# Conv and gate columns of a hybrid decoder step by pairs in seven block products

## The chip, the cores and the metric

The kernel runs on one core of a Trainium2 chip. A core has TensorE (matrix products; in the profile PE, its weight loads PEld), VectorE (DVE), ScalarE (ACT), GpSimd (POOL) and SyncE (SP), each with a queue of its own that it works off in order, and 16 DMA engines. Transfers are issued by SP and by Pool. The metric is the time of one execution on the device in microseconds (us).

## The reference, cut to what matters

One step of a decoder layer for 560 tokens: 16 meta tokens, 512 prompt tokens and 32 sample tokens (8 sequences of 4). The model width is 2048; attention and convolution have 1024 channels.

```
h = rmsnorm(x, g_pre)
q, k, v, ga, cb, cc, ch, gc, ma, mc = jnp.split(h @ w_in, split_offsets(), axis=-1)
a = attend(q, k, v, b_sb).reshape(bsz, t, D_ATTN) * jax.nn.silu(ga)
u = cc * ch
u_ext = jnp.concatenate([conv_hist.astype(u.dtype), u], axis=1)
c = cb * causal_conv(u_ext, w_conv, b_conv) * jax.nn.silu(gc)
merged = (jax.nn.sigmoid(ma + b_gate[:D_MODEL]) * (a @ w_pa)
          + jax.nn.sigmoid(mc + b_gate[D_MODEL:]) * (c @ w_pc))
y = x + rmsnorm(merged @ w_out, g_post)
```

Columns q to gc are 1024 wide each, ma and mc 2048. The attention has 8 heads of 128 and is stick-breaking: a weight is a sigmoid times the product of (1 - sigmoid) of all later keys before the query, computed by sums of softplus. Sample tokens also attend to 512 cached keys of their sequence, in four pages of 128 that a page table names. All is float32. The meta tokens' outputs are dropped.

## The kernel before

**Products.** Channels lie on the partitions, tokens along the free axis. A number is kept as hi + lo, and a product is three matmuls: whi by hi, whi by lo, wlo by hi. A weight tile is a block of 1024 rows by 128 columns (512 KB): weights() (L180 to L191) loads it on SP into one of three raw tiles, ScalarE casts hi (L188), VectorE subtracts to get lo (L189), four such pairs at most. A column tile of h @ w_in takes two such blocks: for each of two halves of the tokens (a PSUM block each; some 272 columns), 16 contraction tiles with three matmuls (gemm_into, L201). That is 96 matmuls per column tile. PSUM has three blocks for such products (mm), three for logits (z), one for o and one for transposes.

**Order.** RMSNorm and its split into h_hi, h_lo; the ga columns; eight heads (head(), L336 to L465: K, V and Q columns, logits L396, softplus, sums L450, product with V L460, result to a_scr in DRAM L465); then conv_in(0), whose columns stand beside the last head; the gate columns (L659 to L666); convolution; a @ w_pa and c @ w_pc by pairs of column tiles (L716 to L735); the output product (16 column tiles for tokens below 288, the rest by token, L796 to L840) and the last norm. A scheduler lays the instructions of each engine out in advance; each engine then keeps that order.

**Decode.** decode_steps() is a generator, and dec_step() advances it beside the projections. Each of 32 pages of keys (512 KB, Pool queue, L527 to L535) is multiplied with the four queries of its sequence (qb, q rows broadcast to all partitions, L546): for two queries by a VectorE product 1024 wide (pr, L553) that ScalarE sums by head (junk, L556), for two by VectorE product-and-sum by head (prod, L560). This lies at the gate columns, one step for each column tile. Then softplus and exponent of the logits, and 32 pages of values with 128-row products (L631), beside the columns of the convolution.

**Gates and convolution.** A gate tile is sigmoid of its PSUM block, and goes to gate_scr in DRAM by Pool (L666). conv_in(i) makes cc and ch columns, their product u and the three taps; later gc and cb columns (L684 to L691) finish c in SBUF (c_raw), which is split into c_hl (L703). a_hl is read back from a_scr two tiles at a time beside the last four of these (arl).

Of the kernel before, what the change touches and what calls it, by code (L numbers as in the profile page):

```python
# [8 lines left out]
F32 = mybir.dt.float32  # L9
F32R = mybir.dt.float32r  # L10
# [15 lines left out]
MID = 288                # tokens [.., MID) and [MID, T) go to two PSUM banks  # L26
ALL = ((0, MID), (MID, T))
QRY = ((NMETA, MID), (MID, T))           # tokens whose outputs are asked for
CNV = ((NMETA - 2, MID), (MID, T))       # these and the conv history before them
TQ = T - NMETA           # 544  # L30
PQ = SEQ                 # prompt tokens among them
# [5 lines left out]
EPS = 1e-6  # L37
LNEXP = "natural_log_exp_and_others"
# [6 lines left out]
def hybrid_step_kernel(  # L45
# [38 lines left out]
    # -------------------------------------------------------------- constants  # L84
# [17 lines left out]
    def load_x(xt, i):  # L102
        lo, hi = XT[i]
        if i == 0:
            nc.sync.dma_start(xt[0:NMETA, :], meta_tokens)
            nc.sync.dma_start(xt[NMETA:hi, :], xp[0:hi - NMETA, :])
        elif hi <= TP:
            nc.sync.dma_start(xt, xp[lo - NMETA:hi - NMETA, :])
        else:
            nc.sync.dma_start(xt[0:TP - lo, :], xp[lo - NMETA:SEQ, :])  # L110
            nc.sync.dma_start(xt[TP - lo:hi - lo, :], xs)
# [21 lines left out]
    # g_pre on every partition, by a product with ones  # L133
# [85 lines left out]
    def parts(outs, ranges, base=0):  # L219
        """(PSUM block, slice of a tile whose column 0 is token `base`) of each range."""  # L220
        return [(o, slice(t0 - base, t1 - base)) for o, (t0, t1) in zip(outs, ranges)]

    # the first two gates start on the first tokens while the others are normalized
    START = ((NMETA, 2 * P), (2 * P, T))
# [21 lines left out]
    # small tables: per-channel columns by a transpose of row-wise loads  # L246
# [88 lines left out]
    def head(h):  # L335
# [18 lines left out]
        for ob, s in parts(o, ALL):  # L354
            act.copy(vr[:, s], ob)
# [515 lines left out]
```

## Time and profile before

| | |
|---|---|
| median of 3 runs | 1734.3 us (1733.22 to 1734.79) |
| span of the profiled execution | 1736.9 us |
| TensorE busy | 1706.4 us, 12764 matmuls recorded |
| VectorE, ScalarE, GpSimd busy | 842.8, 744.7, 202.2 us |
| DMA, mean over the span | 249.87 MB, 144 GB/s |

The profiled execution is 2.6 us above the median of the timed runs. A row of instruction groups reads: line of the kernel, engine, operation, output<-inputs, shapes, count | busy us, mean ns of one | idle time of the engine just before them, and what ended most of it. A row of a window has its start and end, its length, then busy us and count for PE, PEld, DVE, ACT and POOL, the granted clock of TensorE (1.00 is full), the mean share of the DMA engines, and GB/s. A row of the timeline has start, length, engine, line, operation and tiles. Matmuls overlap in the pipeline, so their rate is read from counts in a window, not from the length of one.

### The profile page before, as it was taken

What the parts mean: (1) busy time and instruction counts of PE and PEld (TensorE: products, weight loads), DVE (VectorE), ACT (ScalarE), POOL (GpSimd) and SP (SyncE); (2) the same over time, 40 slices, a digit from 0 to 9 for tenths busy, and PEclk for the clock granted to TensorE, in tenths of its full rate; (3) what the DMA queues carried; (4) which work ended last, traced back from release to release, by engine and by line L of the source; (5) the groups of instructions that cost most, each with busy time, mean ns of one, the idle gap of its engine ahead of it and who ended that gap; (6) DMA issues with size and microseconds to landing.
All of it is one profiled execution on the core that took longest, in us unless ns stands there. A gap on an engine that the chain in (4) does not pass through costs nothing.

```text
span 1736.9 us, 32151 instructions
## 1 busy us (share of the span) xinstructions
PE 1706.4 (98%) x12764; PEld 1637.0 (94%) x12764; DVE 842.8 (49%) x2092; ACT 744.7 (43%) x2026; POOL 202.2 (12%) x345
## 2 busy tenths in 40 slices
PE   5999999999999999999999999999999999999997
PEld 4999999999999999999999878899999999999986
DVE  7322554554445999996123222242224554444464
ACT  4322555455454999886223111132223222244543
POOL 5000222122111111111001111010000000000010
PEclk9999999999999999999999999999999999999999
DMA  6333333333325777774343444343233444567584
GB/s 191 94 110 116 88 99 93 87 88 98 99 82 192 247 257 253 248 244 148 111 120 102 166 160 149 121 139 91 80 98 85 137 127 133 164 166 184 174 260 153
DMA packets 302057, 249.87 MB, mean 144 GB/s; under 512 B 9181, under 2 KB 272145, under 8 KB 298721
## 3 DMA queue, kind: packets, MB, share of 16 engines
q1 hardware_dynamic: 278992, 161.89, 32.0%
q0 software_dynamic: 22912, 85.91, 14.2%
q8 instruction: 100, 1.64, 0.4%
q14 instruction: 51, 0.42, 0.1%
q10 hardware_dynamic: 2, 0.01, 0.0%
HBM read 225.42 MB, written 22.36 MB: 143 GB/s over the span
## 4 chain that ended last, share of the span: by engine, by line
PE 95%; DVE 2%; DMA 2%; ACT 0%; issue 0%; SPq 0%; POOLq 0%; POOL 0%; ACTq 0%; DVEq 0%
PE mm L201 83%; PE z L631 2%; PE z L830 2%; PE mm L830 2%; PE z L450 1%; DMA raw<-in_w_out 1%; PE o L460 1%; PE z L396 1%; PE o L830 1%; DMA raw<-in_w_in 1%; DVE hn L164 0%; PE tp L830 0%; PE tp L316 0%; DVE h_lo L177 0%; PE z L785 0%; DVE rtmp L120 0%
## 5 line engine op out<-in xcount | busy, mean ns | idle before, releaser
L201 PE MATMUL mm<-h_hi,wlo 128*128 128x272 f32 (+4 forms) x3072 | 894.1, 291 | 0.0
L201 PE MATMUL mm<-h_hi,whi 128*128 128x272 f32 (+4 forms) x3072 | 892.9, 291 | 0.0
L201 PE MATMUL mm<-h_lo,whi 128*128 128x272 f32 (+4 forms) x3072 | 888.1, 289 | 0.3 <-DVE h_lo L177 0.2
L201 PEld LDWEIGHTS mm<-h_hi,whi 128*128 128x128 f32 x3072 | 580.7, 189 | 9.3 <-issue 6.7
L201 PEld LDWEIGHTS mm<-h_hi,wlo 128*128 128x128 f32 x3072 | 580.0, 189 | 4.1 <-issue 3.4
L201 PEld LDWEIGHTS mm<-h_lo,whi 128*128 128x128 f32 x3072 | 579.2, 189 | 4.8 <-issue 3.4
L189 DVE TENSOR_TENSOR wlo<-raw,whi 128x1024 fp32r<-128x1024 f32 x252 | 308.4, 1224 | 493.7 <-ACT whi L188 492.3
L188 ACT CAST whi<-raw 128x1024 fp32r<-128x1024 f32 x256 | 269.0, 1051 | 518.0 <-PE mm L201 499.8
L556 ACT ACTIVATE junk<-pr 128x128 f32<-128x128 f32 x512 | 150.7, 298 | 7.1 <-DVE pr L553 4.3
L560 DVE CUSTOM_DVE_ANT_0 prod<-page,qb 128x128 f32<-128x128 f32 x512 | 116.2, 285 | 1.0 <-DMA qb<-q_scr 1.0
L201 PE MATMUL mm<-m,whi 128*128 128x288 f32 x512 | 105.8, 301 | 0.0
L556 ACT ACTIVATION_READ_ACCUMULATOR junk<-pr 128x1 f32 x512 | 97.2, 190 | 0.0
L201 PE MATMUL mm<-c_hl,whi 128*128 128x272 f32 x512 | 96.8, 287 | 0.0
L201 PE MATMUL mm<-a_hl,whi 128*128 128x272 f32 x512 | 96.7, 288 | 0.0
L201 PEld LDWEIGHTS mm<-m,whi 128*128 128x128 f32 x512 | 84.0, 193 | 0.0
L553 DVE TENSOR_TENSOR pr<-page,qb 128x1024 f32<-128x1024 f32 x64 | 78.0, 1220 | 6.2 <-ACT junk L556 5.7
L201 PEld LDWEIGHTS mm<-c_hl,whi 128*128 128x128 f32 x512 | 80.7, 188 | 0.0
L201 PEld LDWEIGHTS mm<-a_hl,whi 128*128 128x128 f32 x512 | 80.5, 189 | 0.0
L201 PE MATMUL mm<-m,wlo 128*128 128x288 f32 x256 | 76.6, 299 | 0.0
L201 PE MATMUL mm<-c_hl,wlo 128*128 128x272 f32 x256 | 74.2, 290 | 0.0
L201 PE MATMUL mm<-a_hl,wlo 128*128 128x272 f32 x256 | 73.9, 289 | 0.0
L804 DVE TENSOR_TENSOR wlo<-raw,whi 128x1024 fp32r<-128x1024 f32 x32 | 39.1, 1224 | 38.4 <-ACT whi L803 37.9
(289 smaller groups left out, 1641.6 us busy)
## 6 DMA issues: line engine op xcount, KB each, us to landing
raw<-in_w_in SPq DMA_DIRECT2D x192, 512.0 KB, 3.9
raw<-in_w_out SPq DMA_DIRECT2D x64, 512.0 KB, 4.0
qb<-q_scr POOLq DMA_DIRECT2D x16, 1024.0 KB, 7.1
page<-in_cache_k POOLq DMA_DIRECT2D x32, 512.0 KB, 6.0
page<-in_cache_v POOLq DMA_DIRECT2D x32, 512.0 KB, 5.4
gate_scr<-gt POOLq DMA_DIRECT2D x16, 544.0 KB, 4.6
gt<-gate_scr POOLq DMA_DIRECT2D x16, 544.0 KB, 5.1
raw<-in_w_pa SPq DMA_DIRECT2D x16, 512.0 KB, 3.9
```

The lines of the kernel that those rows point to most:

```text
L188: act.copy(hi, raw)
L189: lo_eng.tensor_sub(lo, raw, hi.bitcast(F32))
L201: pe.matmul(o, lhsT=w, rhs=r[:, t0:t1], start=(k == 0 and n == 0), stop=(k == nk - 1 and n == 2))
L396: pe.matmul(zt[:m, c0:c0 + n], lhsT=l[:, s0:s0 + m], rhs=r[:, ts:ts + n], start=(c0 == 0 and i == 0), stop=(i == 2), skip_group_check=True)
L450: pe.matmul(o, lhsT=l, rhs=x, start=False, stop=(i == len(ops) - 1), skip_group_check=True)
L460: pe.matmul(ot[:, ts - NMETA:ts - NMETA + n], lhsT=l[:m, st, :], rhs=x[:m, c0:c0 + n], start=False, stop=(g == GROUPS[-1] and i == 2), ski ...
L553: dve.tensor_mul(pr, kt, qb[0][:, t, :])
L556: act.activation(junk, pr[:, h * P:(h + 1) * P], AF.Copy, accum_out=z_all[:, pg, b, h, t:t + 1])
L560: dve.tensor_tensor_reduce(out=prod, in0=kt[:, h * P:(h + 1) * P], in1=qb[t // 2][:, t % 2, h * P:(h + 1) * P], scale=1.0, scalar=0.0, op0 ...
L631: pe.matmul(po[hf][32 * j:32 * (j + 1), :], lhsT=lhs, rhs=rhs, start=(pg == 0), stop=(pg == NPG), tile_position=(0, 32 * j), skip_group_ch ...
L804: dve.tensor_sub(lo, raw, hi.bitcast(F32))
L830: pe.matmul(po[i], lhsT=l, rhs=r, start=(k == 0 and q == 0), stop=(k == KD - 1 and q == 2))
```

## The change

**Pairs.** h is cut into four blocks: two halves of the channels by two halves of the tokens (280 each: 8 meta tokens and 272 others, so both halves ask for the same number of outputs). Two neighbouring column tiles of w_in are four weight blocks w11, w12, w21, w22 (the first index is the column tile, the second the half of the channels). The 2 x 2 product takes seven block products instead of eight, with sums of weight blocks and sums of h blocks:

```diff
+        s = sp2.tile([P, 8, P], F32, name="s", bufs=2)
+        nc.sync.dma_start(s, win[k1, c2].rearrange("(k p) c -> p k c", p=P))
+        w_add(s, win[k2, c2])
+        w11, w21 = w_load(win[k1, c1]), w_load(win[k1, c2])
+        w_add(w21, win[k1, c1])
+        w12, w22 = w_load(win[k2, c1]), w_load(win[k2, c2])
...
+        product(x, w_split(w11), rb(0, 0), True, False)
+        product(q, w_split(s), rb(0, 1), True, False)
+        act.activation(y, x, AF.Copy, scale=-1.0)
+        dve.tensor_add(s, s, w11)
+        product(y, w_split(s), rt(0), False, False)
+        s5 = tmp("s5")
+        act.copy(s5, q)
+        product(x, w_split(w12), rb(1, 0), False, True)
+        s2 = tmp("s2")
+        act.copy(s2, y)
+        yield 0, 0, x
+        product(y, w_split(w21), rt(1), False, False)
+        c22 = tmp("c")
+        dve.tensor_sub(c22, y, s5)
+        yield 1, 1, c22
+        dve.tensor_add(s, s, w12)
+        product(q, w_split(s), rb(1, 1), False, True)
+        c12 = tmp("c")
+        dve.tensor_sub(c12, q, s2)
+        yield 0, 1, c12
+        product(y, w_split(w22), rt(2), False, True)
+        yield 1, 0, y
...
+    def w_add(dst, src):
+
+        pool.dma_start(dst, src.rearrange("(k p) c -> p k c", p=P), accum_op=ALU.add)
```

product() is 8 contraction tiles by three matmuls (L713 of the new kernel); x and q are mm blocks of PSUM, y is o. w_split is a ScalarE cast (L681) and a VectorE subtraction (L682). Two of the four weight sums are made by loads that add into the tile (w_add, L687, Pool queue), two by VectorE (L723, L735). The raw tiles become five instead of three, the split ones three instead of four. The sums of h blocks (t_hi, t_lo, three of each) are made once ahead of the pairs by VectorE and ScalarE, and the block of the first channels and second tokens of h is rewritten with a difference. The first four gate column tiles (gate_one) stay whole and stand beside that; 16 pairs then make cc, ch, gc and cb of two channel tiles at a time, 14 pairs the other gates.

**Other moves.**

```diff
-    wraw = ctx.enter_context(tc.tile_pool(name="wraw", bufs=3))
-    whl = ctx.enter_context(tc.tile_pool(name="whl", bufs=4))
+    wraw = ctx.enter_context(tc.tile_pool(name="wraw", bufs=5))
+    whl = ctx.enter_context(tc.tile_pool(name="whl", bufs=3))
...
+                for b in range(DB):
+                    for tp_ in range(2):
...
+                        for pg in range(NPG):
+                            kt = d1.tile([P, 512], F32, name="kpage", bufs=3)
+                            page_load(kt, kc, b, pg, cs)
...
+        n_group[0] += 1
+        if n_group[0] % 5:
+            dec_step(1, "logits")
...
+        for m in range(2):
+            pool.dma_start(c_scr[i + m], ys[m])
...
+    for k in range(8):
+        cr = g3.tile([P, 2, TQ], F32, tag="gt", name="cr")[:, 0, :]
+        pool.dma_start(cr, c_scr[k])
+        split_evac(c_hl[:, k, :], c_hl[:, 8 + k, :], cr, cr)
...
+    for j in range(KD):
+        cs = slice(j * P, (j + 1) * P)
+        gt = g3.tile([P, 2, TQ], F32, tag="gt", name="gt")[:, 1, :]
+        pool.dma_start(gt, gate_scr[j][:, 1, :])
+        oc = gemm(weights([w_pc[0][:, cs]]), lambda k: (c_hl[:, k, :], c_hl[:, 8 + k, :]), QH)
+        for ob, s in qparts(oc):
+            dve.tensor_mul(gt[:, s], ob, gt[:, s])
+        pool.dma_start(gate_scr[j][:, 1, :], gt)
+        dec_step(2)
...
+    for k in range(8):
+        ar = g3.tile([P, 2, TQ], F32, tag="gt", name="ar")[:, 0, :]
+        pool.dma_start(ar[:, 0:PQ], a_scr[k])
+        dve.tensor_copy(ar[:, PQ:TQ], a_s[:, k, :])
+        split_evac(a_hl[:, k, :], a_hl[:, 8 + k, :], ar, ar)
```

The key pages are read by halves of the heads, 512 columns, each half twice (once for each two queries), in 16 steps spread over the pairs: the counter lets four of five groups through. c goes through DRAM (c_scr). The w_pc products come first, alone, with the softplus of the decode and the value pages beside them, and put gate times product back to gate_scr; after the decode's end a is read back and the w_pa products follow. conv_in(0) no longer exists, so nothing of the convolution stands beside the last head; in the output product the last column chunk is worked for both token tiles by turns.

TensorE at the end of the last head: before, the product with V (L460) has rows of conv_in's columns (L201, mm) between its own.

```order
L201 MATMUL mm<-h_lo,whi 128x272
L201 MATMUL mm<-h_hi,wlo 128x272
L201 MATMUL mm<-h_hi,whi 128x272
L460 MATMUL o<-hi_5613,vhi 128x400
L201 MATMUL mm<-h_lo,whi 128x272
L201 MATMUL mm<-h_hi,wlo 128x272
L201 MATMUL mm<-h_hi,whi 128x272
L201 MATMUL mm<-h_lo,whi 128x272
L201 MATMUL mm<-h_hi,wlo 128x272
L460 MATMUL o<-lo_5614,vhi 128x400
L460 MATMUL o<-hi_5613,vlo 128x400
```

After, at the same place, the last column rows (L203) come first, then the sums (now L459) and the product with V (now L469) follow each other; the first rows of the next column tile stand behind the last of them.

```order
L459 MATMUL z<-hi_5570,neg_one 128x16
L459 MATMUL z<-lo_5571,neg_one 128x16
L459 MATMUL z<-e_5600,neg_one 128x400
L469 MATMUL o<-hi_5644,vhi 128x400
L469 MATMUL o<-lo_5645,vhi 128x400
L469 MATMUL o<-hi_5644,vlo 128x400
L469 MATMUL o<-hi_5644,vhi 128x16
L469 MATMUL o<-lo_5645,vhi 128x16
```

What moved is the filling: between the last logits and L459 there are 90 column rows, behind it none.

VectorE within one pair of the convolution in the new kernel: low parts of weights (L682), the two weight sums (L723, L735), and the decode's products (L544 pr, L553 prod).

```order
L682 TENSOR_TENSOR wlo<-s,whi 128x1024
L553 ISA prod,z_all<-kpage,qb 128x128
L553 ISA z_all 128x1
L553 ISA prod,z_all<-kpage,qb 128x128
L553 ISA z_all 128x1
L682 TENSOR_TENSOR wlo<-raw,whi 128x1024
L735 TENSOR_TENSOR s<-s,raw 128x1024
L544 TENSOR_TENSOR pr<-kpage,qb 128x512
L682 TENSOR_TENSOR wlo<-raw,whi 128x1024
L544 TENSOR_TENSOR pr<-kpage,qb 128x512
L682 TENSOR_TENSOR wlo<-s,whi 128x1024
```

Before, L553 and L560 stood beside the gate columns alone, with L189 between them; the sums are new.

Pool's queue in the new kernel from the last pairs into the w_pc stage: adding loads (L687), gates out (L744), c back (L865), pages of values (L524; an ISA row reads the page's number).

```order
L687 DMA s<-in_w_in 128x8x128
L744 DMA gate_scr<-g 128x544 x2
L687 DMA raw<-in_w_in 128x8x128
L744 DMA gate_scr<-g 128x544 x3
L865 DMA cr<-c_scr 128x544 x2
L744 DMA gate_scr<-g 128x544
L865 DMA cr<-c_scr 128x544 x2
L612 DMA v_new<-v_scr 32x1024
L524 ISA
L524 DMA vpage<-in_cache_v 128x1024
```

Before, no row of c stood on this queue. Now four more pages of values follow the one shown, and only then the fifth read of c.

More of the change, by code (lines that the diff above doesn't have):

```diff
@@ L37 @@
 EPS = 1e-6
+SCRATCH = 4096
 LNEXP = "natural_log_exp_and_others"
@@ L469, in hybrid_step_kernel @@
         sg = hp.tile([P, TQ], F32, name="sg", bufs=2)
-        for ob, s in parts(o, START if h < 2 else QRY, NMETA):
+        if h < 2:
+            c = HC - 2 * P
+            blocks = ((o[0], slice(0, 2 * P - HM)), (o[1][:, 0:c], slice(2 * P - HM, HQ)),
+                      (o[1][:, c + HM:], slice(HQ, TQ)))
+        else:
+            blocks = qparts(o)
+        for ob, s in blocks:
             act.activation(sg[:, s], ob, AF.Silu)
@@ new lines, in dec_step, with dec_group, w_load @@
+            if dec_at[0] in ("end", until) and dec_at[0] is not None:
+                return
+            dec_at[0] = next(dec, "end")
+    n_group = [0]
+    def dec_group():
+        n_group[0] += 1
+        if n_group[0] % 5:
+            dec_step(1, "logits")
+    gctx = ExitStack()
+    gp = gctx.enter_context(tc.tile_pool(name="gates", bufs=2))
+    sp2 = gctx.enter_context(tc.tile_pool(name="sums", bufs=1))
+    def w_load(src):
+        raw = wraw.tile([P, 8, P], F32, tag="raw", name="raw")
+        nc.sync.dma_start(raw, src.rearrange("(k p) c -> p k c", p=P))
+        return raw
@@ new lines, in hybrid_step_kernel @@
+    for i in range(0, 8, 2):
+        conv_pair(i)
+    for j in range(2, KD, 2):
+        for w, c in ((0, COL_MA), (1, COL_MC)):
+            gs = [gp.tile([P, 2, HU], F32, tag="cv", name="g", bufs=3).rearrange("p a b -> p (a b)")[:, 0:TQ] for _ in range(2)]
+            for m, half, b in pair(c + j * P, HQ):
+                act.activation(gs[m][:, by_query(m, half)], b, AF.Sigmoid, bias=gate_bias(j + m, w))
+            for m in range(2):
+                gate_out(j + m, w, gs[m])
+            dec_group()
@@ new lines, in hybrid_step_kernel @@
+    m2 = ap_.tile([P, KD, TQ], F32R, tag="m2", name="m2")
+    for j in range(KD):
+        cs = slice(j * P, (j + 1) * P)
+        gt = g3.tile([P, 2, TQ], F32, tag="gt", name="gt")
+        pool.dma_start(gt, gate_scr[j])
+        oa = gemm(weights([w_pa[0][:, cs]]), lambda k: (a_hl[:, k, :], a_hl[:, 8 + k, :]), QH)
+        mt = m1 if j < 8 else m2
+        for ob, s in qparts(oa):
+            dve.tensor_mul(gt[:, 0, s], ob, gt[:, 0, s])
+            dve.tensor_add(gt[:, 0, s], gt[:, 0, s], gt[:, 1, s])
+            split_evac(mt[:, j % 8, s], mt[:, 8 + j % 8, s], gt[:, 0, s], gt[:, 0, s])
```

378 lines of the change are left out of this document (206 added, 172 removed).

## The prediction

> **What bounds the kernel now.** The page first: busy shares, then the chain that ended last.
>
> ```profile
> span 1736.9 us, 32151 instructions
> PE 1706.4 (98%) x12764; PEld 1637.0 (94%) x12764; DVE 842.8 (49%) x2092; ACT 744.7 (43%) x2026; POOL 202.2 (12%) x345
> PE 95%; DVE 2%; DMA 2%; ACT 0%; issue 0%; SPq 0%; POOLq 0%; POOL 0%; ACTq 0%; DVEq 0%
> L189 DVE TENSOR_TENSOR wlo<-raw,whi 128x1024 fp32r<-128x1024 f32 x252 | 308.4, 1224 | 493.7 <-ACT whi L188 492.3
> L188 ACT CAST whi<-raw 128x1024 fp32r<-128x1024 f32 x256 | 269.0, 1051 | 518.0 <-PE mm L201 499.8
> L556 ACT ACTIVATE junk<-pr 128x128 f32<-128x128 f32 x512 | 150.7, 298 | 7.1 <-DVE pr L553 4.3
> ```
>
> TensorE is the bound nearly everywhere; casts and splits of weights wait for it. So a matmul taken away is worth its full issue time, as long as nothing else takes its place. How much the others have left differs by stage, so I read the windows next: the K pages of the decode beside gate tiles (560 to 790), the V pages (965 to 1140), a plain stretch of projections (1140 to 1325), and the start of the pa/pc stage (1325).
>
> ```profile
> core 0: us, PE busy (x) PEld busy (x) DVE busy (x) ACT busy (x) POOL busy (x), PEclk, DMA share, GB/s
> 560.00:790.00 230.00, 230.00 (x1828) 230.00 (x1827) 219.95 (x1072) 206.51 (x1100) 28.04 (x52) 1.00 0.74 248
> 965.00:1140.00 175.00, 175.00 (x1207) 140.76 (x1206) 47.00 (x84) 32.08 (x59) 19.84 (x37) 1.00 0.44 146
> 1140.00:1325.00 185.00, 185.00 (x1473) 185.00 (x1472) 55.30 (x76) 43.28 (x56) 6.45 (x12) 1.00 0.35 102
> 1325.00:1340.00 15.00, 15.00 (x122) 15.00 (x121) 8.67 (x13) 7.53 (x11) 0.00 (x0) 1.00 0.31 88
> ```
>
> In the K stage VectorE is busy 96% of the time and ScalarE 90%, and TensorE still never stalls: a full engine off the path costs nothing while TensorE has work. From the plain stretch come two prices. One matmul of 272 columns issues every 185/1473 = **0.1256 us**. A weight load of 512 KB serves 48 matmuls, so 30.7 loads took at most 0.35 x 185 = 64.8 us of all 16 DMA engines, 2.1 us each; I take **1.9**, since eight reads of a_scr also lie there (about 6 us, estimated).
>
> **What the change removes.** 30 pairs each save one block product of 24 matmuls: 720 x 0.1256 = **-90.4 us**. That is the whole gain. A pair is 168 matmuls, 21.1 us; all 30 pairs are 633 us where 723 stood.
>
> **What it adds, engine by engine, in those 21.1 us.** The durations of VectorE come from start to start in the timeline:
>
> ```profile
> 600.02 0.28 DVE L560 CUSTOM_DVE_ANT_0 prod<-page,qb 128x128 f32<-128x128 f32 x1
> 600.23 0.08 DVE L560 DVE_READ_ACCUMULATOR2_ANT z_all<- 128x1 f32 x1
> ...
> 603.71 1.22 DVE L189 TENSOR_TENSOR wlo<-raw,whi 128x1024 fp32r<-128x1024 f32 x1
> 604.85 0.28 DVE L560 CUSTOM_DVE_ANT_0 prod<-page,qb 128x128 f32<-128x128 f32 x1
> ```
>
> A 1024-wide pass takes 1.14 us, a prod 0.21, a 512-wide pr about 0.6 (half a pass, estimated). A pair has 7 low parts and 2 sums (9 x 1.14 = 10.3) and two PSUM differences (0.35 each, estimated): 11.0. A decode step has 8 half pages: 8 pr and 32 prod, 4.8 + 6.7 = 11.5. By the code four of five pairs carry a step; pairs of the convolution add its taps (about 2 us per pair). So **VectorE** is at 11.0 + 0.8 x 11.5 + 1 = 21.2 of 21.1 if the steps stay in 20 pairs; the order spreads them to about pair 26, which leaves 93 to 95%. **ScalarE**: 7 casts at 1.05, 7 PSUM reads at about 0.4, 32 junk at 0.3 for four fifths of the pairs: 17.8, 84%.
>
> **DMA**, the same way:
>
> ```profile
> raw<-in_w_in SPq DMA_DIRECT2D x192, 512.0 KB, 3.9
> page<-in_cache_k POOLq DMA_DIRECT2D x32, 512.0 KB, 6.0
> qb<-q_scr POOLq DMA_DIRECT2D x16, 1024.0 KB, 7.1
> gate_scr<-gt POOLq DMA_DIRECT2D x16, 544.0 KB, 4.6
> 560.00:570.00 10.00, 10.00 (x81) 10.00 (x80) 10.00 (x56) 8.87 (x50) 0.54 (x1) 1.00 1.03 372
> ```
>
> Seven weight loads per pair, two of them adding into the tile: 7 x 1.9 = 13.4. The old K stage moved 33.5 MB of pages and q rows and some 5 MB of gates beside 38 weight loads; 0.74 x 230 = 170 us less 38 x 1.9 leaves 97.5 us, 394 GB/s. Each page half is now read twice, 50.3 MB, 128 us over some 24.5 pairs: 5.2; gates 1.4. Sum **20.0 of 21.1 us, 95%**, if an adding load costs what a plain one does. No row of before shows an adding load. From below it is not cheaper than a plain one (it moves the same bytes in); from above I take twice, since it also reads its destination. The nearest row is the plain weight load, which has the same rows of 512 bytes, so the sum uses its price. The last row shows that a share of 1.03 for ten microseconds stalled nothing.
>
> The Trainium skill speaks against that price: "Collectives: The Full Stack", section "The bandwidth ceiling: the fold count and why AG ≠ RS ≠ AR", says that a DMA that reduces needs two source reads and gets half the rate of a copy, 32.35 against 62.28 GB/s there. By that rule the adding loads are at the upper end; no run here shows it, and it is the second rival below.
>
> The sum of waits in the pair stage: three engines between 84 and 95% with in-order queues. On Pool a half page that waits for VectorE to free one of three buffers holds the next adding load behind it, that holds the split, and that TensorE. I put **+15** (0 to 50): half a microsecond per pair.
>
> **Stages at the edges.** The last head, then the seams.
>
> ```profile
> 508.42 0.39 PE L396 MATMUL z<-qhi,klo 128*128 128x512 f32 x1
> ...
> 521.56 0.39 PE L450 MATMUL z<-hi,neg_u 128*128 128x512 f32 x1
> ...
> 542.70 0.39 PE L460 MATMUL o<-hi,vlo 128*128 128x512 f32 x1
> ```
>
> Before, the last head needed 34 us from its last logits to its last product with V, and 210 matmuls of conv_in (26 us) filled it. After, the order has 90 (11 us) ahead of L459 and none behind. 120 x 0.1256 = 15 us are uncovered; some 6 us of that chain were casts and splits that no longer stand in it; 3 are added for the clock: **+12** (5 to 22).
>
> What a stall costs beyond itself:
>
> ```profile
> 1575.68 0.29 PE L201 MATMUL mm<-m,wlo 128*128 128x288 f32 x1
> 1578.83 0.87 PE L785 MATMUL z<-ident,orw 128*96 128x128 f32 x3 [2.85 <-ACT orw L782]
> 1578.00:1582.00 4.00, 3.17 (x14) 3.15 (x15) 2.96 (x3) 2.81 (x9) 0.22 (x1) 0.50 0.29 76
> 1582.00:1586.00 4.00, 4.00 (x23) 4.00 (x22) 1.10 (x1) 1.34 (x2) 0.29 (x1) 0.65 0.75 223
> 1586.00:1590.00 4.00, 4.00 (x33) 4.00 (x32) 1.39 (x3) 2.15 (x7) 0.00 (x0) 1.00 0.46 131
> ```
>
> One idle stretch of 2.85 us was followed by a granted clock of 0.50 and then 0.65 before it was whole again: 2.0 + 1.4 us lost. So three edges with a stall pay about 3 us each, and they are in my figures for the edges.
>
> The Trainium skill, "TensorE: Matmul & The Clock Gate", "Part 1: The HAM clock gate (the "warmup" mystery)", asks for an idle window of about 3.4 us before the clock falls. Here 2.85 us did it, so the measurement decides; by the rule alone, edges broken into waits under 3.4 us would keep the clock, and the sum would be 9 us lower.
>
> **The conv seam.** c_hl takes h's place, so all eight channel tiles are read back from c_scr after the last pair, through two buffers. On Pool the last gate's write stands ahead of loads 3 and 4, and v_new and five V pages (2.6 MB, 7 us at 372 GB/s) ahead of loads 5 to 8. Before, c lay in SBUF, and 1325:1340 has no idle time. Last evacuation 1, gate write 4.6, pages 7, four loads and splits about 6: 19 us, less 9 of matmuls that go ahead by k, plus 3 for the clock: **+15** (5 to 22).
>
> **The a seam** is built alike: a_hl after the last V step, eight reads through two gate buffers that must first be written back. Before, they were spread over gc/cb tiles. Four rounds of read and split, 4 us each, plus the write-back, less what k order hides: **+15** (5 to 18).
>
> **V pages.** In 965:1140, 175 us hold 1207 matmuls that would take 152 at the plain rate, so V matmuls already cost 23 us there. Now the pages come singly between the shorter pc products, and the softplus of the logits lies there too: **+8** (0 to 30).
>
> **Small terms**, each bounded by about its double: sums of h, which the order puts partly ahead of the heads, +2 (VectorE has more to do while the first tokens are split); rewriting h's block ahead of the first pair +2 (a cast and a subtraction of 2192 elements, some 4.4 us, beside a product of 3.0); three split buffers in place of four in the heads +3; the two token tiles of the last chunk ending together +3.
>
> **Sum.** 2 + 12 + 2 + 15 + 15 + 8 + 15 + 3 + 3 = +75. 1736.9 - 90.4 + 75 = 1721.5 on the profiled execution, which stood 2.6 above the median of the runs shown (1734.3): **1719 us**, its own range 1697 to 1733.
>
> **Rivals.**
> 1. *The edges hide themselves.* The k order lets TensorE run while the tiles come, and the pairs absorb waits as the old K stage did. Last head 5, pairs 5, both seams 15, V 0, small terms 10: +35, so **1679**. For it: 96% VectorE without a stall in 560:790. Against: that stage had no adding loads and four split buffers.
> 2. *An adding load costs two plain ones* (slower). 13.4 + 3.8 + 5.2 + 1.4 = 23.8 us of DMA in a pair of 21.1: 2.7 x 24.5 pairs = 66 in place of my 15: **1770**. DMA becomes the bound from about 1.3 times the plain price; the kernel is slower than before from about 1.6 times (3.0 us). Against: the 1.03 row, and the pairs after the pages' end have slack.
> 3. *VectorE's order.* At 95% with an in-order queue, a pr or prod that waits for its page holds the split behind it. If bubbles are a tenth of its decode pairs, 22.4 us per pair: 1.3 x 24.5 = 32 instead of 15: **1736**, no change.
> That the change doesn't do what it says is excluded: the order has 30 x 168 rows of L713.
>
> **Chances.** Forecast 0.45, hidden edges 0.15, adding loads 0.25, VectorE 0.15. A measurement of this kernel can tell about 0.2% (3.5 us) from no change. Faster by more: 0.15 + most of 0.45 + a little of the third, 0.60; within: 0.10; slower: 0.30. The range reaches from the first rival to just past the second, 1676 to 1775.
>
> **What would show it.** Pairs at 21.1 us with no idle of TensorE before L713: the gain is there. A DMA share near 1.0 through the pairs, with TensorE waiting for splits whose release is the adding load on s or w21: rival 2. The same waits with VectorE full and DMA under 0.95: rival 3. TensorE idle of 10 us at the end of the last head and at both seams, with a granted clock under 1: my edge terms; none: rival 1. I am wrong altogether if 272-column matmuls into interleaved PSUM blocks issue at another pace than 0.1256, or if Pool's many small issues delay the weights.

## The result, and the profile after

The changed kernel takes 1880.9 us (median of 4 runs, 1873.4 to 1887.1) against 1733.8 us before: a ratio of 1.085, 95% interval 1.082 to 1.088. It is slower; the forecast of 1719 us missed by 162 us. The profiled execution has a span of 1885.5 us. In the experiments below a time with a ratio is the median of several runs; a span alone is that of a single run.

The page of the changed kernel: span, busy shares, and the chain that ended last.

```profile
span 1885.5 us, 32282 instructions
PE 1707.2 (91%) x12044; PEld 1603.9 (85%) x12044; DVE 1071.5 (57%) x2388; ACT 902.4 (48%) x2231; POOL 409.2 (22%) x590
PE 29%; DMA 17%; DVE 8%; issue 7%; ACT 1%; POOL 1%; POOLq 0%; DVEq 0%; ACTq 0%; SPq 0%
```

TensorE was 95% of the chain and is 29% of what is shown of it now; DMA holds 17%, VectorE 8%. It has 720 fewer matmuls and yet is busy just as long (1707.2 against 1706.4 us), since it counts as busy at a lower clock too. Where that happens, the windows tell: last head, pairs with key pages, pairs without, c seam, value pages, a seam.

```profile
core 0: us, PE busy (x) PEld busy (x) DVE busy (x) ACT busy (x) POOL busy (x), PEclk, DMA share, GB/s
500.00:550.00 50.00, 39.93 (x254) 35.12 (x254) 19.52 (x35) 19.29 (x35) 9.11 (x17) 0.83 0.26 65
600.00:1200.00 600.00, 504.74 (x3669) 496.24 (x3668) 443.83 (x1360) 368.67 (x1208) 172.66 (x220) 0.91 0.90 216
1300.00:1350.00 50.00, 50.00 (x400) 50.00 (x399) 27.01 (x25) 22.60 (x32) 10.37 (x9) 1.00 0.93 198
1350.00:1400.00 50.00, 38.38 (x259) 35.88 (x258) 28.33 (x37) 30.92 (x40) 11.54 (x20) 0.83 0.61 196
1436.00:1546.00 110.00, 110.00 (x545) 60.38 (x543) 17.15 (x32) 9.89 (x11) 22.92 (x43) 1.00 0.63 209
1550.00:1600.00 50.00, 39.17 (x261) 36.63 (x261) 23.05 (x54) 12.59 (x19) 9.64 (x18) 0.86 0.55 163
```

Pairs without key pages (1300 to 1350) run at 400 matmuls in 50 us, 0.125 us each: a pair is 21 us and TensorE never waits, as worked out. Pairs with key pages run at 3669 in 600 us, 0.164 each, so 27.5 us. All L713 rows together stand between 582 and 1377 us: the pair stage is **795 us** long where 5040 matmuls need 633, so **162 us** are lost in it. (The length of this stage, from its first product to its last, is the measure in all experiments below.) All other stages together cost 77 us more than before (148.6 us more span, and the 90.4 us that the products save, less these 162); the forecast had 60 for them.

What TensorE, VectorE and Pool waited for, from the groups of the page and of the view that keeps shapes apart:

```profile
L713 PE MATMUL o<-t_hi,whi 128*128 128x272 f32 (+1 forms) x720 | 225.6, 313 | 69.0 <-DVE c L733 56.0
L553 DVE CUSTOM_DVE_ANT_0 prod<-kpage,qb 128x128 f32<-128x128 f32 x512 | 126.3, 284 | 85.7 <-DMA kpage<-in_cache_k 85.7
L544 DVE TENSOR_TENSOR pr<-kpage,qb 128x512 f32<-128x512 f32 x128 | 85.9, 686 | 80.6 <-DMA kpage<-in_cache_k 78.7 <-ACT junk L550 1.3 <-ACT ln L826 0.4
...
L687 POOL DMA_DIRECT2D raw<-in_w_in x30 | 48.7, 1622 | 162.7 <-DMA raw<-in_w_in 61.0 <-ACT junk L550 35.4 <-DVE z_all L553 25.9
L687 POOL DMA_DIRECT2D s<-in_w_in x30 | 48.4, 1612 | 188.3 <-DMA s<-in_w_in 64.1 <-ACT junk L550 51.8 <-issue 21.8
```

TensorE seems to wait for VectorE's subtraction c22 (L733). But VectorE itself sat idle 85.7 + 78.7 = 164 us for half pages of keys, as much as the stage lost: its queue is in order, and the subtraction stands behind them. It also has little to make up for it with: 443.8 us busy in 600 are 20.3 us of work per pair, where TensorE needs 21.1. One such stall in the timeline, Pool first, then VectorE, then TensorE:

```profile
1102.70 0.54 POOL L524 DMA_DIRECT2D kpage<-in_cache_k  x1
1111.52 1.61 POOL L687 DMA_DIRECT2D raw<-in_w_in  x1 [8.27 <-DMA raw<-in_w_in]
1112.45 1.81 POOL L524 DMA_DIRECT2D kpage<-in_cache_k  x2
...
1122.79 0.69 DVE L544 TENSOR_TENSOR pr<-kpage,qb 128x512 f32<-128x512 f32 x1 [8.20 <-DMA kpage<-in_cache_k]
1124.04 1.22 DVE L682 TENSOR_TENSOR wlo<-raw,whi 128x1024 fp32r<-128x1024 f32 x1
1125.78 0.43 DVE L733 TENSOR_TENSOR c<-o,s 128x272 f32<-128x272 f32 x1
...
1126.35 0.57 PE L713 MATMUL o<-t_hi,whi 128*128 128x272 f32 x1 [7.27 <-ACT whi L681]
```

Pool waits 8.3 us for the plain load of w21 to land before it may issue the load that adds to it; the key pages behind it go out at 1112.5 and are there at 1122.8; VectorE idles 8.2 us, then works off a page and a split before c22; TensorE idles 7.3 us. (The view names a cast, long done, as the releaser there; the instruction that ended just before is c22.) So there are two candidates: what the adding loads cost the DMA engines, and the order in which Pool and VectorE must take things.

### The profile page after: what moved, and what is told of

Same layout as the page of the kernel before. It is cut to its first block, busy times and chain, and to the rows that moved or that the text cites. A ratio compares the mean times of both kernels' runs of the same rounds, so it can differ in the third digit from the quotient of the medians.

```text
span 1885.5 us, 32282 instructions
## 1 busy us (share of the span) xinstructions
PE 1707.2 (91%) x12044; PEld 1603.9 (85%) x12044; DVE 1071.5 (57%) x2388; ACT 902.4 (48%) x2231; POOL 409.2 (22%) x590
## 3 DMA queue, kind: packets, MB, share of 16 engines
q0 software_dynamic: 97648, 147.80, 31.7%
## 4 chain that ended last, share of the span: by engine, by line
PE 29%; DMA 17%; DVE 8%; issue 7%; ACT 1%; POOL 1%; POOLq 0%; DVEq 0%; ACTq 0%; SPq 0%
PE mm L203 15%; DMA kpage<-in_cache_k 10%; PE mm L713 3%; DMA s<-in_w_in 3%; PE z L631 3%; PE o L713 3%; DMA raw<-in_w_in 2%; DVE wlo L682 2%; PE z L1000 2%; DVE prod L553 2%; PE mm L1000 1%; DVE pr L544 1%; DMA ar<-a_scr 1%; DVE s L723 1%; PE o L1000 1%
## 5 line engine op out<-in xcount | busy, mean ns | idle before, releaser
L203 PE MATMUL mm<-h_hi,whi 128*128 128x272 f32 (+3 forms) x1152 | 338.7, 294 | 7.9 <-ACT g L754 5.3
L203 PE MATMUL mm<-h_lo,whi 128*128 128x272 f32 (+3 forms) x1152 | 337.9, 294 | 0.2 <-DVE h_lo L179 0.2
L203 PE MATMUL mm<-h_hi,wlo 128*128 128x272 f32 (+3 forms) x1152 | 337.4, 294 | 0.0
L713 PE MATMUL mm<-h_hi,wlo 128*128 128x272 f32 (+1 forms) x960 | 280.3, 292 | 11.4 <-DVE wlo L682 11.2
L713 PE MATMUL o<-t_hi,whi 128*128 128x272 f32 (+1 forms) x720 | 225.6, 313 | 69.0 <-DVE c L733 56.0
L713 PE MATMUL mm<-h_hi,whi 128*128 128x272 f32 (+1 forms) x960 | 280.3, 292 | 7.7 <-ACT whi L681 7.6
L713 PE MATMUL mm<-h_lo,whi 128*128 128x272 f32 (+1 forms) x960 | 278.9, 290 | 0.0
L713 PE MATMUL o<-t_hi,wlo 128*128 128x272 f32 (+1 forms) x720 | 222.9, 310 | 22.2 <-DVE wlo L682 22.1
L203 PEld LDWEIGHTS mm<-h_hi,whi 128*128 128x128 f32 x1152 | 220.8, 192 | 9.8 <-ACT g L754 6.0
L713 PE MATMUL o<-t_lo,whi 128*128 128x272 f32 (+1 forms) x720 | 222.1, 308 | 0.0
L203 PEld LDWEIGHTS mm<-h_lo,whi 128*128 128x128 f32 x1152 | 220.2, 191 | 1.1 <-DVE h_lo L179 0.3
L203 PEld LDWEIGHTS mm<-h_hi,wlo 128*128 128x128 f32 x1152 | 220.2, 192 | 0.2
L713 PEld LDWEIGHTS o<-t_hi,whi 128*128 128x128 f32 x720 | 151.1, 210 | 73.0 <-DVE c L733 32.5
L713 PEld LDWEIGHTS mm<-h_hi,wlo 128*128 128x128 f32 x960 | 182.9, 191 | 12.5 <-DVE wlo L682 12.3
L713 PEld LDWEIGHTS mm<-h_hi,whi 128*128 128x128 f32 x960 | 183.3, 191 | 9.7 <-ACT whi L681 9.6
L713 PEld LDWEIGHTS mm<-h_lo,whi 128*128 128x128 f32 x960 | 182.9, 191 | 0.0
L553 DVE CUSTOM_DVE_ANT_0 prod<-kpage,qb 128x128 f32<-128x128 f32 x512 | 126.3, 284 | 85.7 <-DMA kpage<-in_cache_k 85.7
L713 PEld LDWEIGHTS o<-t_hi,wlo 128*128 128x128 f32 x720 | 150.6, 209 | 24.6 <-DVE wlo L682 24.6
L682 DVE TENSOR_TENSOR wlo<-raw,whi 128x1024 fp32r<-128x1024 f32 x120 | 146.3, 1219 | 24.2 <-ACT whi L681 24.1
```

The costliest lines, as they stand in the source:

```text
L203: pe.matmul(o, lhsT=w, rhs=r[:, t0:t1], start=(k == 0 and n == 0), stop=(k == nk - 1 and n == 2))
L553: dve.tensor_tensor_reduce(out=prod, in0=kt[:, hs], in1=qt[:, t, hs], scale=1.0, scalar=0.0, op0=ALU.mult, op1=ALU.add, accum_out=out)
L682: dve.tensor_sub(lo, x, hi.bitcast(F32))
L713: pe.matmul(o, lhsT=l[:, k, :], rhs=r, start=(start and k == 0 and m == 0), stop=(stop and k == 7 and m == 2), skip_group_check=True)
```

## The experiments

Theory A: an adding load costs the DMA engines over twice a plain one, and 25 us of transfers don't fit into 21 us. Theory B: the queues couple, whatever the transfers cost. Later theories are named where they come up.

**Plain loads in place of adding ones.** The instruction order of all engines is that of the changed kernel, row by row.

```diff
-        pool.dma_start(dst, src.rearrange("(k p) c -> p k c", p=P), accum_op=ALU.add)
+        pool.dma_start(dst, src.rearrange("(k p) c -> p k c", p=P))
```

> The two adding loads of a pair become plain loads into the same tiles, so two of the four weight sums are missing from the product; order, queues and waits of every engine stay the same row by row. Theory A (an adding load costs the DMA engines over twice a plain one, 66 ns against 29 ns for a 512-byte packet in the trace of the changed kernel): 4.7 us of DMA go from every pair, pairs with key pages fall from 27.8 us to 21 to 23 us, span 1735 to 1760 us. Theory B (queues: on Pool the adding load waits for the landing of the plain one, key pages stand behind it, on VectorE the weights stand behind the pages): all these waits stay, pairs stay at 26 us or more, span above 1840 us.

Span 1805.2 us, pair stage 716 us, 83 over 633; two of the four weight sums are missing here. The window of the stage, then one of pairs without pages:

```profile
600.00:1200.00 600.00, 548.54 (x4128) 539.40 (x4127) 495.98 (x1529) 410.36 (x1342) 156.41 (x245) 0.97 0.82 243
1240.00:1290.00 50.00, 50.00 (x400) 50.00 (x399) 27.32 (x25) 23.01 (x34) 4.03 (x6) 1.00 0.59 170
```

Half of the loss (79 of 162 us) is the adding alone, so A holds for it; more is left than A said, less than B said. What an adding load costs the DMA engines follows from the row of Pool's queue in the two pages (packets, MB, share of the 16 engines over the span), first of the changed kernel, then of this run:

```profile
q0 software_dynamic: 97648, 147.80, 31.7%
q0 software_dynamic: 43888, 147.80, 25.4%
```

The bytes are the same. 31.7% of 1885.5 us less 25.4% of 1805.2 us are 139 us for 60 loads, **2.3 us each more** than a plain load. The packets say the same: an adding load of 512 KB is 1024 packets of 512 bytes at 66 ns, over 16 engines 4.2 us; SP's plain loads have such packets too, at 29 ns, 1.9 us. That is 2.2 times the plain price. (A plain load from Pool's queue goes in packets of 4 KB, so there are 53760 packets fewer.)

**The four sums on VectorE, from four plain loads.** The blocks that the adding loads fetch are loaded anyway.

```diff
-        w_add(s, win[k2, c2])
...
-        w_add(w21, win[k1, c1])
...
+        w11, w21, w22 = w_load(win[k1, c1]), w_load(win[k1, c2]), w_load(win[k2, c2])
+        dve.tensor_add(s, w21, w22)
+        dve.tensor_add(w21, w21, w11)
+        w12 = w_load(win[k2, c1])
```

> Four plain loads per pair in place of seven loads; all four weight sums are made by VectorE from the tiles that are loaded anyway. Theory A and theory B both take their cause away; what is left is VectorE: 11 passes of 1.14 us, two PSUM differences of 0.43, and about 7.8 us of decode per pair, 21.2 us on the mean and more while a decode step is beside it. Pairs 21.5 to 23.5 us, span 1730 to 1780 us, DMA share about 0.65. If pairs stay above 25 us, neither DMA nor Pool's queue was the cause but VectorE's load.

1768.3 us, ratio 1.019 (1.017 to 1.021); pair stage 682 us, 49 over. With two more VectorE passes per pair the kernel is 113 us faster than the changed one: the adding loads were a bad trade. VectorE is 94% busy in this window and TensorE at 0.136 us per matmul.

```profile
600.00:1200.00 600.00, 572.23 (x4424) 564.82 (x4423) 562.63 (x1536) 425.93 (x1347) 111.90 (x197) 0.99 0.60 184
```

**Two of the sums on Pool.** As above, with pool.tensor_add for the two sums that the loads made.

> As the run with the sums on VectorE, but the two that were adding loads are made by Pool, at 3.3 us each from the four such passes in the trace. Theories A and B: pairs 21.2 to 22 us, span 1720 to 1745 us. If Pool's passes hold VectorE up (both read two SBUF operands), VectorE loses up to 6.6 us per pair and pairs go to 24 us or more; then VectorE's 1024-wide passes are longer than 1.22 us in the trace.

1831.7 us, ratio 1.055 (1.053 to 1.057); pair stage 749 us. Pool's passes hold VectorE up, as the groups of this run show:

```profile
L553 DVE CUSTOM_DVE_ANT_0 prod<-kpage,qb 128x128 f32<-128x128 f32 x512 | 193.0, 416 | 8.2 <-DMA kpage<-in_cache_k 5.7 <-DMA qb<-q_scr 2.5
L682 DVE TENSOR_TENSOR wlo<-raw,whi 128x1024 fp32r<-128x1024 f32 x120 | 174.5, 1454 | 10.6 <-ACT whi L681 10.3
L697 POOL TENSOR_TENSOR raw<-raw 128x1024 f32<-128x1024 f32 x30 | 83.5, 2782 | 1.3
```

A prod takes 416 ns on the mean where it took 289 with these sums on VectorE, a low part from a raw tile 1454 where it took 1222. The Trainium skill ("SBUF — State Buffer", "🔬 SBUF: two separate sides") says that a VectorE operation with two SBUF inputs and a Pool operation that reads SBUF lock a pair of ports against each other for a whole instruction; these rows agree with it, though they show the lengthening and not the lock.

**Each half page loaded once.** Both q tiles of a sequence are held, and a half page serves four queries.

```diff
-                        for pg in range(NPG):
-                            kt = d1.tile([P, 512], F32, name="kpage", bufs=3)
-                            page_load(kt, kc, b, pg, cs)
...
+                    for pg in range(NPG):
+                        kt = d1.tile([P, 512], F32, name="kpage", bufs=3)
+                        page_load(kt, kc, b, pg, cs)
+                        for tp_ in range(2):
```

> Each half page of keys is loaded once, for four queries, in place of twice; adding loads stay. Theory A: DMA per pair falls by 1.7 us of some 25, pairs 25.5 to 26.5 us, span 1830 to 1850 us. Theory B: half of the waits for pages go, pairs 23.5 to 25 us, span under 1820 us.

Span 1884.3 us, pair stage 795 us: no change, so both expectations missed. The DMA share fell from 0.90 to 0.82, and the transfers of a pair (share times length) from 24.7 to 22.9 us, as theory A had it; but VectorE now also waits 51 us for the q rows, whose two buffers are both in use through a step, and with the pages 146 us in all. The run took one wait away and made another, and doesn't decide.

**Key pages on SP's queue**, with adding loads and then with plain ones.

```diff
-        pool.dma_start(t, cache[bass.ds(page_reg[i], 1), :, cs].rearrange("o s c -> (o s) c"))
+        eng.dma_start(t, cache[bass.ds(page_reg[i], 1), :, cs].rearrange("o s c -> (o s) c"))
```

> The half pages of keys are issued by SP in place of Pool; adding loads, bytes and VectorE's work stay. Theory A (price of the adding loads alone, about half of the loss as the plain-load run shows): pairs stay at 27 us or more, span above 1860 us. Theory B (pages stand on Pool behind an adding load that waits for the landing of its plain one, and VectorE behind the pages): pages no longer wait for that, pairs with pages 24 to 25.5 us, span 1800 to 1840 us.

Span 1848.3 us, pair stage 761 us, with the DMA engines nearly full:

```profile
600.00:1200.00 600.00, 522.51 (x3796) 507.81 (x3795) 466.68 (x1443) 386.28 (x1293) 115.16 (x113) 0.94 0.95 228
```

It lies between the theories: 34 us are Pool's order, and what remains runs into a share of 0.95. At 0.158 us per matmul a pair takes 26.6 us, and 0.95 of that is 25 us of transfers, as it was before (0.90 of 27.5).

> Plain loads in place of adding loads (two of four sums missing) and the half pages on SP. If A and B together are the cause, only VectorE's own load is left: pairs 21.2 to 22.5 us, span 1725 to 1765 us. If pairs stay at 24 us as with plain loads alone, Pool's order was not the other half.

Span 1804.3 us, pair stage 717 us: nothing gained over plain loads from Pool. In these runs Pool's order costs only while adding loads stand in it. B in its simple form is out.

**Eight products, all else of the change kept.** pair() becomes two whole column tiles:

```diff
+        for m in range(2):
+            o = proj(c + m * P, ((HC - n, HC), (T - n, T)))
+            for half in range(2):
+                yield m, half, o[half]
```

> Eight products per pair (two whole column tiles with four plain loads, no sums of weights or of h), all else of the change as it is. By the accounting of the stages, everything but the pair stage cost 77 us more than the forecast's 90 us gain leaves: pairs 24.1 us without a stall, span 1800 to 1820 us. If the edges cost what I forecast (60 us), 1795 us or less.

Span 1845.7 us, 109 over the kernel before, more than either figure. So the rest of the change (last head, value pages, seams) costs a good part by itself: w_pc and w_pa stages last from 1341.5 to 1635.5, 294 us, where they took 193 before, of which some 63 are value pages that stood elsewhere before and cost 45 there. In this run the last head also has stalls of 17 us in all, and more differs than the products: the scheduler put the key pages earlier, VectorE works on them from 330 to 768 us, beside the heads, where the changed kernel has them from 592 to 1273. So the 109 us are not the edges of the changed kernel alone.

**Value pages together.** On the run with four sums on VectorE, the matmuls of a group of four pages are made ready at once by a copied operand that depends on the last page.

```diff
+                    al = d2.tile([P, 4, H * DT], F32, name="al", bufs=2)
+                    dve.scalar_tensor_tensor(
+                        out=al, in0=vts[3][:, 0:128].rearrange("p (j x) -> p j x", j=4), scalar=0.0,
+                        in1=A_all[:, pg, 4 * g:4 * g + 4].rearrange("p b h t -> p b (h t)"),
+                        op0=ALU.mult, op1=ALU.add)
...
-                            lhs = A_all[:, pg, bb].rearrange("p h t -> p (h t)")
+                            lhs = al[:, j, :]
```

> The sums on VectorE as before, and the value pages' matmuls made to wait for the fourth page of a group through a copied operand, so that eight stand in a row on TensorE. In the changed kernel 168 matmuls of that stage took some 63 us beside the w_pc products, 45 us in the kernel before. Expected: the w_pc stage shorter by 15 to 30 us, span 1735 to 1750 us; if the stage keeps its length, the density of these matmuls was not its price.

1739.6 us, ratio 1.001 (1.0005 to 1.002). The group in the changed kernel, then in this one:

```profile
L631 PE MATMUL z<-vpage,A_all 128*32 128x512 f32 x128 | 55.2, 598 | 0.0
```

```profile
L636 PE MATMUL z<-vpage,al 128*32 128x512 f32 x128 | 17.1, 656 | 10.8 <-DVE al L623 10.8
```

The same 128 instructions fill 55.2 us of TensorE when those of one page come at a time, and 17.1 us when those of four pages stand in a row, though each lasts no less: pages of one group use different columns of the array, and these run beside each other. They also wait 10.8 us for their operand. As fast as before the change, no faster.

**Less work on VectorE.** 256 of the 512 product-and-sums are left out, from the run with four loads and from that with plain loads.

```diff
+                                    if tp_ == 1 and t == 1:
+                                        continue
```

> The run with the four sums on VectorE, less the product-and-sums of the fourth query of each sequence (256 of 512, 54 us of VectorE; those logits are left at zero). Theory C (with four plain loads VectorE is the bound of the pair stage: 94% busy, 49 us over the 633 of its matmuls): pair stage falls from 682 to 640 to 652 us, span 1722 to 1738 us. If it stays above 670, VectorE's load is not what is left.

> The same 256 product-and-sums left out of the run with plain loads in place of adding ones (pair stage 716 us, two weight sums missing). If what remained there was VectorE's load too, the stage falls by 40 us or more, to 675 or less, span under 1766 us. If it was the pages' late arrival behind seven loads of weights (VectorE waited 87 us for pages), it falls by less than 20, span above 1785 us.

Spans 1766.1 and 1804.6 us, pair stages 685 and 716 us, against 682 and 716 without the cut: nothing gained. But the runs don't refute theory C. The order of the instructions changed with the work: in the first run the key pages are worked off by 1061 us in place of 1227, and while they last VectorE is as full as before (426 us busy from 600 to 1060, against 430). So a pair with pages has as much VectorE work as it had, and is as slow; from the twenty-second on, pairs have no stall. In the second run VectorE waits 88 us for pages, as with plain loads before (87).

**Seams eased**, on the run with value pages together: c back on SP through four buffers of its own, the prompt part of a beside the last eight w_pc products, six buffers for value pages.

```diff
+            cr = crp.tile([P, TQ], F32, name="cr")
+            nc.sync.dma_start(cr, c_scr[k])
...
+        if j >= 8:
+            k = j - 8
+            ar = g3.tile([P, 2, TQ], F32, tag="gt", name="ar")[:, 0, 0:PQ]
+            nc.sync.dma_start(ar, a_scr[k])
+            split_evac(a_hl[:, k, 0:PQ], a_hl[:, 8 + k, 0:PQ], ar, ar)
```

> The run with value pages together, and both seams eased: c is read back on SP's queue through four buffers of its own, the prompt part of a is read and split beside the last eight w_pc products, only the 32 sample columns after the decode, and six buffers for value pages in place of five. The c seam had 11 us of idle in the changed kernel, the a seam 20 in the run before this one. Expected: 20 to 28 us less, span 1713 to 1722 us, faster than the kernel before by about 1%. If the seams were not the price, no change (1741 us).

1718.5 us, ratio 0.989 (0.987 to 0.991): 1.1% faster than the kernel before. The gain came from the a seam, which has no idle time left; at the c seam TensorE's longest wait for c is 5.1 us, as it was before, so there Pool's order was not the price.

**The last product of each pair behind the first of the next** (on the run before; then on the changed kernel with adding loads; then on that with plain loads). y goes to a z bank.

```diff
+        product(x, w_split(w11), rb(0, 0), True, False)
+        flush()
+        product(q, w_split(s), rb(0, 1), True, False)
...
+        def last():
+            product(y, w_split(w22), rt(2), False, True)
+            consume(1, 0, y)
+            after()
+        pend.append(last)
```

> The run with eased seams, and the last product of each pair (w22) put behind the first product of the next pair; the block y lies in a z bank of PSUM. VectorE then has 6 us in place of 3 to read y (c22) before TensorE adds to it again, and ScalarE 6 in place of 3 for y = -x. Theory D (what is left of the pair loss, 50 to 55 us, is TensorE waiting for readers of y that stand behind decode work in VectorE's and ScalarE's queues): pair stage 688 to 645 to 662 us, span 1678 to 1698 us. Theory E (the splits are late, not the readers of y): pair stage above 678 us, span above 1710.

1709.9 us, ratio 0.983 (0.981 to 0.986); pair stage 671 us, from 688. TensorE's waits for the readers of y, 13.4 us for c22 and 8.4 for y = -x in the run before, are gone from the view of waits, and the stage is 17 us shorter. Theory D is right for a third of the 55 us; its figure for the stage was too low. Of the 17 us, 9 arrive in the median; 4 us of idle come back at the a seam.

> The changed kernel with adding loads, with only that deferral. In its trace TensorE waited 56 us in all for c22 on VectorE, which itself stood behind key pages. Theory A (DMA full at a share of 0.90 by the adding loads): the waits move to the splits, pair stage stays above 775 us, span above 1865 us. Theory D: the pair stage falls from 795 to 760 us or less.

> Plain loads in place of adding ones, with the deferral of each pair's last product. Theory F: pages still come late, the wait moves from the readers of y to the splits, stage 705 us or more. Theory D: the readers of y were the wait, stage 660 to 690 us.

Spans 1894.2 and 1826.5 us, pair stages 807 and 740 us: 11 and 24 us worse than without. With adding loads TensorE's waits moved from y to the splits, 55.6 us for the low part (L682) where 22.1 stood. So in these runs slack for the readers helped only where transfers were in time.

**No adding loads at all.** Both lines with w_add are left out; five plain loads per pair remain, and VectorE's passes are those of the changed kernel.

> The adding loads are left out altogether (two of four weight sums missing): five plain loads per pair, VectorE's passes as in the changed kernel. DMA work of a pair with pages falls to about 16.5 us. Theory F (what is left with seven plain loads, 83 us, is lateness of pages and weights that grows with the DMA share of 0.82): stage 645 to 670 us, span 1735 to 1760. Theory G (the static order of the queues, whatever the DMA does): stage above 695 us, span above 1785.

Span 1753.9 us, pair stage 671 us, 38 over 633: theory F's figure for the span, and a microsecond above its figure for the stage. The run takes away the transfers, and with them the second load that s and w21 waited for; it doesn't part the two.

```profile
600.00:1200.00 600.00, 577.81 (x4488) 569.97 (x4487) 520.94 (x1552) 428.23 (x1360) 112.88 (x199) 0.99 0.70 213
```

What VectorE waited for, with plain loads, then here (us in total, times, longest):

```profile
DVE prod L553 <- DMA kpage<-in_cache_k: 46.6, 25, 4.6
DVE pr L544 <- DMA kpage<-in_cache_k: 40.7, 19, 6.9
```

```profile
DVE prod L553 <- DMA kpage<-in_cache_k: 21.6, 13, 3.1
DVE pr L544 <- DMA kpage<-in_cache_k: 16.6, 17, 2.2
DVE prod L553 <- DMA qb<-q_scr: 3.5, 3, 2.1
```

All runs with like passes on VectorE:

| run | DMA share, 600 to 1200 | pair stage | over 633 us | VectorE idle for key pages and q rows |
|---|---|---|---|---|
| the change | 0.90 | 795 | 162 | 164 |
| half pages once | 0.82 | 795 | 162 | 146 |
| pages on SP | 0.95 | 761 | 128 | 121 |
| plain loads | 0.82 | 716 | 83 | 87 |
| plain loads, pages on SP | 0.82 | 717 | 84 | 78 |
| no adding loads | 0.70 | 671 | 38 | 42 |
| the change, last product deferred | 0.87 | 807 | 174 | 163 |
| plain loads, last product deferred | 0.79 | 740 | 107 | 97 |

The share alone doesn't order these runs: 0.82 stands beside 162, 83 and 84 us. The last column does. What the stage loses is, to some 16 us, what VectorE stood idle for rows of the decode: with 19.5 to 20.7 us of work of its own in a pair of 21.1, it can't make an idle good. That the idle is what the loss consists of is read from the agreement of these columns; no run varied it by itself. With the four sums on VectorE it idles only 14 us for such rows, but has 21.4 us of work per pair (562.6 of 600).

## Why the prediction was wrong

**The gain** was as worked out: 720 matmuls less, 0.125 to 0.126 us each, and pairs without pages take 21 us with no stall.

**The step that failed** is the one on the DMA in a pair, "Sum 20.0 of 21.1 us, 95%, if an adding load costs what a plain one does", with the value that I took for that unknown, and the +15 of waits that rests on it. The bounds were plain and twice; the price is 2.2 times, 4.2 us against 1.9, just above the upper one. A pair then has 24.7 us of transfers for 21.1 us of products, and the stage lost 162 us, not 15. That is 147 of the 164 us by which the profiled span (1885.5 against 1721.5) missed: 79 of them go when the adding loads are made plain, and 68 are the +15 itself, too small even at the price that I had taken. I chose by the nearest row, which has the same rows of 512 bytes; but an adding load reads its destination too, and nothing in that row spoke for its being free. The Trainium skill's rule that I cited ("Collectives: The Full Stack", section "The bandwidth ceiling: the fold count and why AG ≠ RS ≠ AR", half the rate for a reduce, told there of rings) came nearer; 66 ns against 29 ns a packet is somewhat less than half the rate.

**Rival 2** had the right cause and nearly the right transfers (23.8 us in a pair, 24.7 measured), but was too cheap: 66 us for the whole overload, 1770 us. Two things were left out. Its transfers were counted as if DMA could be full all the time, where in-order queues leave holes: 34 us went when the pages left Pool's queue, and the share rose from 0.90 to 0.95. And it priced no clock: in the window of the pairs the granted clock is 0.91 on the mean. Of the 3659 starts of matmuls from 600 to 1200 us, 311 follow at 0.22 to 0.30 us, twice the plain interval, and these alone are 32 of the 140 us lost there; the 30 stalls over 0.6 us are 100. I charged 3 us of clock for each of three edges and none for pairs.

**Plain price and 95% full was not good for 15 us either.** Plain loads do make 0.82 of 24.4 us, 20.0 us of transfers per pair, as I had summed, and the stage still lost 83. I read the old K stage as proof that a share of 1.03, with VectorE 96% busy, stalls nothing. In it VectorE waited 1.3 us in all for pages and q rows; here it waits 87 with plain loads. My figure of 95% for VectorE was right (20.2 us of 21.1), and it means that nearly every such wait lengthens the pair. Why pages came in time there and late here was not varied; the buffers, the double reading and the weights in the same queue all differ.

**Rival 3** (VectorE's order) has the path by which the late rows reach TensorE, the wait for c22 behind pages, and rightly the lack of slack. What it lacks is the size: it took bubbles of a tenth, 32 us, where VectorE idled 164, and 77 of these go when the adding loads are made plain.

**A reading of the change** was wrong without harm to the sums: a decode step is four half pages, for two queries, so there are 32 steps and not 16 of eight; the passes per pair come out the same.

**The edges** came near, in part by luck. The last head has 10 us of idle and some 3 of lowered clock, 13 against 12; but only 4.8 us of the idle are the chain of the head. The other 5.3 come after its last product, where the next column tile waits for the first gate's sigmoid (L754) to free a block, which the term didn't have. At the c seam TensorE idles 11.6 of the 33 us from 1377, 4.3 of them for the decode's softplus and not for c; at the a seam 10.8 of the 40 from 1560; with some 6 of lowered clock 29 against 30. **Value pages** cost 18 more than before, 63 against 45 us, where I had 8: the density that I named in the term, and the run with pages together shows it. These make some 60 of the 77 us outside the pair stage; the other 17, where I had 10 in small terms, are not placed.

Left open: what the last 38 us of the pair stage are in the best run, where VectorE is 95% busy (567.1 of 600 us) and no run took work off it at the same order; the idle at the c seam; and whether a deeper page buffer would do what SP's queue did, which wasn't tried.

## What to carry to other kernels

A load that adds is not a load: its DMA price has to be measured before work is moved to it, and when blocks are in SBUF already, two more passes on VectorE were much cheaper here (1768 against 1881 us for the same mathematics). When DMA, VectorE and ScalarE all come out above 80% of a stage, sum their loads first, then follow one in-order queue through the others: the sum says whether it fits, the queue says who stalls. An engine at 95% of a stage has no slack to catch up with, so what it idles for a late transfer is lost. And seven products for eight does pay (ratio 0.983 with sums on VectorE, value pages batched, seams eased and one product deferred), but only after the things around it were put right.

## What the runs showed of the hardware

- A 512-byte packet of an adding DMA into SBUF took 66 ns, of a plain one 29 ns; an adding load of 512 KB about 4.2 us of all 16 engines, where a plain one took 1.9.
- The adding loads went in packets of 512 bytes, plain loads of the same tiles from Pool's queue in packets of 4 KB: 97648 against 43888 packets for the same 147.80 MB.
- Issuing an adding load took Pool 1.62 us, a plain load of the same tile 0.91, a half page 0.55 us where no adding loads stood in the queue and 0.83 us on the mean between them.
- Matmuls 32 columns wide in different columns of the array overlap when they stand in a row: 17.1 us for 128 against 55.2.
- Pool passes of 1024 elements from SBUF took 2.7 to 2.8 us, and lengthened VectorE's small products beside them from 289 to 416 ns on the mean.
